# A float32 decoder layer on one core: parts of x1 side by side, five of seven products with both parts in one matmul, and the source's order on VectorE and ScalarE in two places

## The chip, the core and the metric

The kernel runs on one core of a Trainium2 chip. The metric is the device time of one execution in microseconds (us). TensorE multiplies matrices, VectorE and ScalarE do elementwise work, GpSimd here mostly issues DMAs, and SyncE issues the loads of weights. Each of these engines takes its instructions strictly in the order in which the program has them; one that waits holds all that stand behind it on its engine.

## The reference, cut to what matters

One layer for 512 tokens of width 2048, all in float32:

```python
h = rms_norm(x, attn_norm)
p = h @ w_in                                   # 2048 x 5632
y = concat(spatial_gating, short_conv, dilated_attention)   # all read p
x = x + y @ w_out                              # 2048 x 2048; this x is x1 below
h = rms_norm(x, mlp_norm)
x = x + square(relu(h @ w_mlp_in)) @ w_mlp_out # 2048 x 8192, then 8192 x 2048
```

## The kernel before

Every float32 product is made of three fp32r products: each operand is split into a high part (ScalarE copies it, rounding to fp32r, L242) and a low part (VectorE subtracts the high part, L243), and `mm3` (L154) issues high by high, high by low and low by high. The transposed tokens xT are held on 128 partitions, 16 slices of depth by 512 tokens. Weights come in pieces of two slices of depth (`load_w`, 128 x 2 x 512 numbers), three pieces deep: SyncE loads `wr`, ScalarE makes `wh`, VectorE makes `wl`.

`stream` (from L195 on) is one loop over all pieces of all groups. For piece i it loads piece i+2, issues the matmuls of piece i, and after each of the two slices takes one entry from a list of tasks (`step`); at a group's end it calls the group's `close`, which takes the results out of PSUM. There are six PSUM banks for this, and most groups use four. What is written there is the source's order. A scheduler then sets the order on each engine by its own estimate of times; a task that looks ready early is moved ahead.

The groups in order:

- **w_in**: four groups for q and k, and others. Together with the first group come the loads of xT (`xr`, `x_chunk`, split by `split_x`), and eight loads of x by token (`xn`, 512 KB each, issued on GpSimd) with a square on ScalarE each, for the first norm (`x_tokens`, `x_statistics`).
- **w_out**: its close adds x, which gives x1, and splits x1 times the gain into `xhl`: all high parts, and 32 KB per partition further on all low parts.
- **First product of the MLP** (w1, 8192 columns): a plain group of 512 columns; then 29 groups of 256 columns (`Strassen`), each by seven products of quarter size in place of eight, with 8 matmul steps each; then a plain group of 256 columns. The moving operands of the seven products are quarters of x1 or sums of them (`tt`). In three of the seven (`half` is None, L820) one weight load serves both parts: a matmul over 512 columns (high and low part of x1, 256 tokens each) and one over 256 (low part of the weights). In the other four, `mm3` issues three matmuls over 256 columns. The two parts come out in two halves of a bank and are added by VectorE.
- **Second product** (w2): four chunks of 2048 rows by four groups of 512 columns, each of 8 pieces (two slices of depth, four banks, three matmuls: 24 matmuls over 512 columns a piece, 192 a group). Its moving operand `hid` is made from the first product, read back from DRAM (`hs`, `hr`): `rest` in `hid_tasks` squares and multiplies on VectorE (L879, L880), copies on ScalarE, subtracts on VectorE, 64 times in all. Chunk 0's first half is made during the last group of w1, its second half during chunk 0's first group, and chunk c+1's during the second and third group of chunk c. `close_mlp_out` (L925) adds each bank to `acc`; only then is the bank free for the next group.

Quoted: the products of a Strassen group, and the task that makes one slice of `hid`.

```python
bank, half = ((0, None), (1, None), (2, 0), (3, None), (2, 1), (4, 0), (4, 1))[j]
...
if half is None:
    nc.tensor.matmul(pv, lhsT=h[:, m], rhs=b, start=start, stop=False)
    nc.tensor.matmul(pv[:, 1], lhsT=l[:, m], rhs=b[:, 0], start=False, stop=stop)
else:
    mm3(pv[:, half], (h[:, m], l[:, m]), (b[:, 0], b[:, 1]), start, stop)
...
def rest(n):
    t, k = room.pop(n), ks[n]
    nc.vector.scalar_tensor_tensor(out=t, in0=t, scalar=0.0, in1=t, op0=ALU.max, op1=ALU.mult)
    nc.vector.tensor_tensor(out=t, in0=t, in1=rbc, op=ALU.mult)
    split(d[:, 0, k], d[:, 1, k], t)
    load(n + ahead)
```

Of the kernel before, what the change touches and what calls it, by code (L numbers as in the profile page):

```python
# [9 lines left out]
F32 = mybir.dt.float32  # L10
# [30 lines left out]
def trunk_kernel(  # L41
# [46 lines left out]

    def step():
        if tasks:  # L90
            f = tasks.popleft()
            if f is not None:
                f()
# [28 lines left out]
    xh, xl = xhl[:, 0], xhl[:, 1]  # L122
    rstd = cpool.tile([P, TB], F32, name="rstd")
# [5 lines left out]
    def load_w(src, n, first=False):  # L129
# [5 lines left out]
        if first:  # L135
            for k in range(2):
                nc.sync.dma_start(out=first[0][:, k], in_=first[1][:, k])
                nc.sync.dma_start(out=raw[:, k], in_=src[:, k])
            for k in range(2):
                nc.vector.tensor_copy(out=h[:, k], in_=raw[:, k])  # L140
                split_x(k, first[0][:, k], g_attn)
                nc.vector.tensor_tensor(out=l[:, k], in0=raw[:, k], in1=h[:, k].bitcast(F32), op=ALU.subtract)
            return h, l
# [9 lines left out]
    def mm3(ps, a, b, start, stop):  # L153
        (ah, al), (bh, bl) = a, b  # L154
        nc.tensor.matmul(ps, lhsT=ah, rhs=bh, start=start, stop=False)  # L155
        nc.tensor.matmul(ps, lhsT=ah, rhs=bl, start=False, stop=False)  # L156
        nc.tensor.matmul(ps, lhsT=al, rhs=bh, start=False, stop=stop)  # L157
# [18 lines left out]
    def tr_group(src, nt, mov, close, order=None, before=None, tail=False):  # L176
# [13 lines left out]
        def mm(k, h, l, which=None):  # L190
            for n, (j, ts) in enumerate(parts):
                if which in (None, n):
                    s = slice(j * P, (j + 1) * P)
                    a, b = mov(order[k])
                    mm3(st[n][:, ts], (h[:, s], l[:, s]), (a[:, ts], b[:, ts]), k == 0, k == KT - 1)  # L195
# [49 lines left out]
    def split_x(k, src, gain):  # L245

        nc.scalar.activation(out=xh[:, k], in_=src, func=AF.Copy, scale=gain[:, k:k + 1])
        nc.vector.scalar_tensor_tensor(
            out=xl[:, k], in0=src, scalar=gain[:, k:k + 1], in1=xh[:, k].bitcast(F32), op0=ALU.mult, op1=ALU.subtract,
        )  # L250
# [13 lines left out]
    def x_tokens(i):  # L264
# [3 lines left out]
        nc.gpsimd.dma_start(out=xn_t, in_=xn_v[:, t, half * DH:(half + 1) * DH])  # L268
        return lambda: nc.scalar.activation(out=xn_t, in_=xn_t, func=AF.Square, accum_out=tok[:, t, half:half + 1])
# [104 lines left out]
    def x_chunk(kp):  # L374
# [6 lines left out]
        for n in range(2):  # L381
            split_x(2 * kp + n, xr[:, n], g_attn)
# [21 lines left out]
    def evac_qk(pss, which, half):  # L404
        gain = q_gain if which == 0 else k_gain
# [322 lines left out]
    def close_out(pss, ng):  # L728

        xg = mlp["xg"]  # L730
        for j in range(4):
# [7 lines left out]
            split_x(n, xg[:, n], g_mlp)  # L739
            tasks.append(lambda n=n: nc.scalar.activation(out=xg[:, n], in_=xg[:, n], func=AF.Copy, scale=g_mlp[:, n:n + 1]))  # L740
        if ng == 3:
            yc["cm"].__exit__(None, None, None)
            mlp["tcm"] = pool("sums")
            tt = mlp["tt"] = mlp["tcm"].__enter__().tile([P, 2, 4, KT // 2, TH], F32R, name="tt")
# [9 lines left out]
    def x_sums(tt, xv, m, j):  # L754
# [5 lines left out]
        split(tt[:, 0, j, s], tt[:, 1, j, s], out)  # L760

    def x_operand(j, m):

        if j < 3:
            k, t = ((0, 0), (1, 0), (1, 1))[j]
            return xhl[:, :, 2 * m + k, t * TH:(t + 1) * TH]
        return mlp["tt"][:, :, j - 3, m]

    class Strassen:
# [41 lines left out]
        def product(self, j, h, l):  # L811
            sp, i = mlp["spool"], self.i
            bank, half = ((0, None), (1, None), (2, 0), (3, None), (2, 1), (4, 0), (4, 1))[j]
# [16 lines left out]

            if j == 0:
# [3 lines left out]
                nc.scalar.copy(out=self.p[0], in_=pv[:, 0])  # L835
                add(self.p[0], pv[:, 1], self.p[0])
                return
            c = self.c
            if j == 1:
                add(c[:, 2], pv[:, 0], self.p[0])  # L840
                add(c[:, 2], pv[:, 1], c[:, 2])
            elif j == 2:
                add(c[:, 0], pv[:, 0], self.p[0])
            elif j == 3:
                nc.scalar.copy(out=self.p[1], in_=pv[:, 0])
                add(self.p[1], pv[:, 1], self.p[1])
            elif j == 4:
                add(c[:, 1], pv[:, 1], c[:, 0])
                add(c[:, 0:6:5], self.p[1].unsqueeze(1).broadcast_to([P, 2, TH]), c[:, 0:2])
            elif j == 6:  # L850
                add(c[:, 3:5], pv, c[:, 0:2])
                for n in range(2):
                    nc.gpsimd.dma_start(out=hd[self.c0 // P + n], in_=c[:, 2 + 2 * n:4 + 2 * n].rearrange("p h t -> p (h t)"))

    def close_mlp_in(pss, f0):

        for j, ps in enumerate(pss):
# [3 lines left out]
            nc.scalar.copy(out=c, in_=ps.rearrange("p (h t) -> p h t", h=2))  # L861
# [5 lines left out]
    def hid_tasks(c, ks, alloc, ahead):  # L867
# [9 lines left out]
        def rest(n):  # L877
            t, k = room.pop(n), ks[n]
            nc.vector.scalar_tensor_tensor(out=t, in0=t, scalar=0.0, in1=t, op0=ALU.max, op1=ALU.mult)  # L879
            nc.vector.tensor_tensor(out=t, in0=t, in1=rbc, op=ALU.mult)  # L880
# [7 lines left out]
    def open_last_in():  # L888
        mlp["tcm"].__exit__(None, None, None)
# [32 lines left out]
    def close_mlp_out(pss, ng):  # L922
        for j in range(4):
            dst = mlp["acc"][:, 4 * ng + j]
            nc.vector.tensor_tensor(out=dst, in0=pss[j], in1=dst, op=ALU.add)  # L925

    def close_last(pss, ng, j, ts):
        dst = mlp["acc"][:, 4 * ng + j, ts]
        nc.vector.tensor_tensor(out=dst, in0=pss, in1=dst, op=ALU.add)
# [22 lines left out]
    groups.append(tr_group(w1[:, :, :T], 4, xmov, lambda pss: close_mlp_in(pss, 0)))  # L952
    for c0 in range(T, DFF - 2 * P, 2 * P):
        groups.append(Strassen(c0))
    groups.append(tr_group(
        w1[:, :, DFF - 2 * P:], 2, xmov, lambda pss: close_last_in(pss, DFF // P - 2), before=open_last_in,
    ))
    for c in range(nch):
        for ng in range(4):
# [6 lines left out]
            ))  # L966
    stream(groups)
# [46 lines left out]
```

## Time and profile before

| | |
|---|---|
| median of 3 runs | 2099.56 us (2097.77 to 2105.01) |
| the profiled execution | 2101.5 us, of which the span from the first to the last instruction is 2099.8 us |
| TensorE busy | 98% of the span |
| VectorE busy | 55% of the span |
| ScalarE busy | 32% of the span |
| mean granted TensorE clock | 0.992 of full speed |

Busy time of TensorE counts matmuls that overlap, so 98% does not say that TensorE runs at its peak; what one matmul costs is read from the distance between the starts of two neighbours in the timeline. Waits of TensorE stand in the list of waits: who waited, for whom, us in total, how often, the longest.

### The profile page before, as it was taken

The numbers are of one execution on the slowest core, as the hardware profiler recorded it, in microseconds if no ns is written. First come the engines' busy times: TensorE is split into PE (matmuls) and PEld (weight loads), VectorE is DVE, ScalarE is ACT, GpSimd is POOL, SyncE is SP. The second block draws the span as 40 slices with busy tenths as digits, with TensorE's granted clock in tenths as the row PEclk, the third lists the DMA queues.
The fourth block names the chain that finished last, engine by engine and source line by source line (L and its number), as shares of the span: only waits on it lengthen the run. The fifth ranks groups of instructions, "written<-read, shape, count | busy, mean of one in ns | idle before, by whom it ended". The sixth has DMA issues, their size and how long they took to land.

```text
span 2099.8 us, 27447 instructions
## 1 busy us (share of the span) xinstructions
PE 2067.3 (98%) x11202; PEld 1807.8 (86%) x11202; DVE 1145.1 (55%) x1530; ACT 674.7 (32%) x905; POOL 100.6 (5%) x194
## 2 busy tenths in 40 slices
PE   9999999999999999999999999999989998999999
PEld 8999888888888889999999999977878887888888
DVE  5443453534335578878888788767372254322222
ACT  6233442322234434334333343432221222221221
POOL 1000000100000000000000000131010010000000
PEclk9999999999999999999999999999999999999999
DMA  8223222433533454444444444474343343233332
GB/s 276 90 76 111 71 71 68 128 96 96 188 119 126 125 161 131 131 140 122 140 131 124 138 131 126 127 254 151 112 150 96 95 133 112 92 101 97 114 120 81
DMA packets 247023, 259.81 MB, mean 124 GB/s; under 512 B 11748, under 2 KB 179940, under 8 KB 246896
## 3 DMA queue, kind: packets, MB, share of 16 engines
q1 hardware_dynamic: 229888, 206.08, 32.6%
q0 software_dynamic: 14560, 47.75, 6.5%
q10 hardware_dynamic: 2448, 4.23, 0.6%
q8 instruction: 88, 1.44, 0.3%
q14 instruction: 39, 0.32, 0.0%
HBM read 232.81 MB, written 25.19 MB: 123 GB/s over the span
## 4 chain that ended last, share of the span: by engine, by line
PE 79%; issue 16%; DMA 3%; POOL 1%; DVE 1%; SPq 0%; ACT 0%; POOLq 0%; DVEq 0%; ACTq 0%
PE pt L155 17%; PE pt L156 17%; PE pt L157 17%; PE pt L823 8%; PE pn L155 5%; PE pn L157 5%; PE pn L156 5%; PE pt L824 4%; DMA hs<-hd 1%; POOL hs L875 1%; DMA hd<-cn 1%; PE sc L505 0%; DMA wr<-in_w_in_dram 0%; PE et L518 0%; DVE wl L243 0%
## 5 line engine op out<-in xcount | busy, mean ns | idle before, releaser
L243 DVE TENSOR_TENSOR wl<-wr,wh 128x1024 fp32r<-128x1024 f32 (+2 forms) x287 | 321.4, 1120 | 652.8 <-ACT wh L242 596.5
L242 ACT CAST wh<-wr 128x1024 fp32r<-128x1024 f32 (+2 forms) x287 | 277.8, 968 | 799.6 <-PE pt L156 661.9
L155 PE MATMUL pt<-xhl,wh 128*128 128x512 f32 (+1 forms) x1144 | 419.6, 367 | 6.0 <-DVE acc L925 6.0
L156 PE MATMUL pt<-xhl,wh 128*128 128x512 f32 (+1 forms) x1144 | 418.3, 366 | 0.0
L157 PE MATMUL pt<-xhl,wl 128*128 128x512 f32 (+1 forms) x1144 | 418.1, 365 | 0.0
L155 PEld LDWEIGHTS pt<-xhl,wh 128*128 128x128 f32 x1144 | 216.5, 189 | 41.3 <-DVE acc L925 6.4
L157 PEld LDWEIGHTS pt<-xhl,wl 128*128 128x128 f32 x1144 | 216.4, 189 | 34.7
L156 PEld LDWEIGHTS pt<-xhl,wh 128*128 128x128 f32 x1144 | 216.6, 189 | 34.4 <-issue 0.2
L242 ACT CAST wh<-wq 128x1024 fp32r<-128x1024 f32 x145 | 152.0, 1048 | 250.7 <-PE pt L156 146.1
L243 DVE TENSOR_TENSOR wl<-wq,wh 128x1024 fp32r<-128x1024 f32 x145 | 177.0, 1221 | 91.2 <-ACT wh L242 91.1
L155 PE MATMUL pt<-hid,wh 128*128 128x512 f32 x512 | 201.7, 394 | 14.7 <-DVE acc L925 14.7
L157 PE MATMUL pt<-hid,wl 128*128 128x512 f32 x512 | 201.3, 393 | 2.1 <-DVE wl L243 2.0
L156 PE MATMUL pt<-hid,wh 128*128 128x512 f32 x512 | 201.2, 393 | 0.0
L155 PE MATMUL pt<-tt,wh 128*128 128x256 f32 x696 | 197.0, 283 | 0.3 <-DVE c L829 0.3
L157 PE MATMUL pt<-tt,wl 128*128 128x256 f32 x696 | 197.1, 283 | 0.0
L156 PE MATMUL pt<-tt,wh 128*128 128x256 f32 x696 | 197.0, 283 | 0.0
L155 PE MATMUL pn<-wh,xhl 128*128 128x384 f32 (+2 forms) x512 | 187.3, 368 | 4.4 <-DVE wh L140 3.8
L156 PE MATMUL pn<-wl,xhl 128*128 128x384 f32 (+2 forms) x512 | 180.4, 352 | 0.0
L157 PE MATMUL pn<-wh,xhl 128*128 128x384 f32 (+2 forms) x512 | 180.2, 352 | 0.0
L823 PE MATMUL pt<-xhl,wh 128*128 128x512 f32 x464 | 165.2, 398 | 0.0
L155 PEld LDWEIGHTS pt<-tt,wh 128*128 128x128 f32 x696 | 132.7, 191 | 3.1 <-issue 0.6
L157 PEld LDWEIGHTS pt<-tt,wl 128*128 128x128 f32 x696 | 132.9, 191 | 0.0
(210 smaller groups left out, 2933.5 us busy)
## 6 DMA issues: line engine op xcount, KB each, us to landing
wr<-in_w_mlp_out_dram SPq DMA_DIRECT2D x128, 512.0 KB, 3.6
wq<-in_w_mlp_in_dram SPq DMA_DIRECT2D x116, 512.0 KB, 4.1
wr<-in_w_in_dram SPq DMA_DIRECT2D x144, 128.0 KB, 2.4
wr<-in_w_out_dram SPq DMA_DIRECT2D x32, 512.0 KB, 3.6
hd<-c POOLq DMA_DIRECT2D x58, 256.0 KB, 2.6
hs<-hd POOLq DMA_DIRECT2D x56, 256.0 KB, 3.4
wr<-in_w_in_dram SPq DMA_DIRECT2D x24, 512.0 KB, 3.5
wr<-in_w_in_dram SPq DMA_DIRECT2D x31, 384.0 KB, 3.2
```

The costliest lines, as they stand in the source:

```text
L155: nc.tensor.matmul(ps, lhsT=ah, rhs=bh, start=start, stop=False)
L156: nc.tensor.matmul(ps, lhsT=ah, rhs=bl, start=False, stop=False)
L157: nc.tensor.matmul(ps, lhsT=al, rhs=bh, start=False, stop=stop)
L242: nc.scalar.copy(out=dst_h, in_=src)
L243: nc.vector.tensor_tensor(out=dst_l, in0=src, in1=dst_h.bitcast(F32), op=ALU.subtract)
L823: nc.tensor.matmul(pv, lhsT=h[:, m], rhs=b, start=start, stop=False)
L824: nc.tensor.matmul(pv[:, 1], lhsT=l[:, m], rhs=b[:, 0], start=False, stop=stop)
L875: nc.gpsimd.dma_start(out=room[n], in_=hd[c * KC + ks[n]])
```

## The change

Three things are done.

1. **Order.** `keep_in_program_order` makes an instruction keep the source's order on its engine. It is set for the VectorE and ScalarE work of splits, `rest`, `close_mlp_out`, `close_last`, `close_mlp_in` and the squares of `xn`, from the start of the stream until the first group closes, and again from the opening of the last group of w1 to the end. The eight `xn` loads are no longer issued ahead: task i issues load i, behind the last matmul that has been issued by then (`behind`), and square i-2. They begin with the sixth piece of the first group, one a piece.
2. **x1's parts side by side.** `xhl` is read as `x1v` in the first product of the MLP: for each slice and each half of the tokens 256 high parts and, right behind, 256 low parts, so a product with both parts reads 512 numbers in a row. The sums `tt` are laid out likewise. The two plain groups of w1 (288 matmuls over 512 columns) now read two runs of 256 numbers, 2 KB from the start of one to the start of the next (`x1mov`).
3. **Five products with both.** Products 0 to 4 of a Strassen group have one matmul over 512 columns and one over 256 for each step; products 5 and 6 keep three over 256. Products 2 and 4 get banks of their own, six in all, and one addition more each on VectorE (`take`).

```diff
+    def ordr(ins):
+        return tc.keep_in_program_order(ins) if ordered[0] else ins
...
+    x1v = xhl.rearrange("p s k t -> p (s k t)").rearrange("p (k h s t) -> p k h s t", k=KT, h=2, s=2)
...
+    def behind(ins):
+
+        tc.add_manual_dep(
+            ins.ins, last[0].ins.name, mybir.DependencyInfo(mybir.DependencyClass.Sync, mybir.DependencyReason.DATA),
+            reason="behind",
+        )
+        return ins
...
     def split(dst_h, dst_l, src):
-        nc.scalar.copy(out=dst_h, in_=src)
-        nc.vector.tensor_tensor(out=dst_l, in0=src, in1=dst_h.bitcast(F32), op=ALU.subtract)
...
+        ordr(nc.scalar.copy(out=dst_h, in_=src))
+        ordr(nc.vector.tensor_tensor(out=dst_l, in0=src, in1=dst_h.bitcast(F32), op=ALU.subtract))
...
-        squares = [x_tokens(i) for i in range(3)]
+        squares = []
 
         def one(i):
-            squares[i]()
-            if i + 3 < 2 * TB:
-                squares.append(x_tokens(i + 3))
-
-        for i in range(2 * TB):
+            if i < 2 * TB:
+                squares.append(x_tokens(i))
+            if i >= 2:
+                squares[i - 2]()
+
+        for i in range(2 * TB + 2):
             tasks.extend([lambda i=i: one(i), None])
         tasks.append(stat_columns)
...
     def evac_qk(pss, which, half):
+        ordered[0] = False
...
+    def x1mov(k):
+        return x1v[:, k, :, 0], x1v[:, k, :, 1]
...
-            bank, half = ((0, None), (1, None), (2, 0), (3, None), (2, 1), (4, 0), (4, 1))[j]
+            bank, half = j if j < 5 else 5, j - 5 if j >= 5 else None
...
+            def take(out, more):
+                add(out, pv[:, 0], more)
+                add(out, pv[:, 1], out)
...
             elif j == 2:
-                add(c[:, 0], pv[:, 0], self.p[0])
-            elif j == 3:
-                nc.scalar.copy(out=self.p[1], in_=pv[:, 0])
-                add(self.p[1], pv[:, 1], self.p[1])
+                take(c[:, 0], self.p[0])
             elif j == 4:
-                add(c[:, 1], pv[:, 1], c[:, 0])
+                take(c[:, 1], c[:, 0])
...
     def open_last_in():
+        ordered[0] = True
...
-            nc.vector.tensor_tensor(out=dst, in0=pss[j], in1=dst, op=ALU.add)
+            ordr(nc.vector.tensor_tensor(out=dst, in0=pss[j], in1=dst, op=ALU.add))
```

What it does to the order is seen at three places. **First, ScalarE at the start of the program.** `xr0` is the first chunk of xT with its two slices, `xn0` the first load by token, `wh2` and `wh3` the high parts of the second and third piece. Before:

```order
L115 ACTIVATE scr_82<-ones_75 128x1
L247 ACTIVATE xhl_93<-xr0_190,par_73 128x512
L269 ACTIVATE xn0_414,tok_99<-xn0_414 128x1024
L247 ACTIVATE xhl_93<-xr0_190,par_73 128x512
L247 ACTIVATE xhl_93<-xr1_206,par_73 128x512 x2
L242 CAST wh2_213<-wr2_212 128x2x384
```

Now:

```order
L120 ACTIVATE scr_82<-ones_75 128x1
L267 ACTIVATE xhl_93<-xr0_190,par_73 128x512 x2
L267 ACTIVATE xhl_93<-xr1_206,par_73 128x512 x2
L262 CAST wh2_213<-wr2_212 128x2x384
L267 ACTIVATE xhl_93<-xr2_218,par_73 128x512 x2
```

The square of `xn0` has gone from between the two slices of the first chunk; all eight squares stand behind `wh11`, the high part of the tenth piece.

**Second, VectorE at the end of the first group of the second product** (`pt265_0` to `_3` are its banks, `hs280` to `hs289` slices of `hid` for the next chunk, `wl275` to `wl277` low parts of the coming pieces). Before:

```order
L879 SCALAR_TENSOR_TENSOR hs287_12654<-hs287_12654 128x512
L880 TENSOR_TENSOR hs287_12654<-hs287_12654,rbc_96 128x512
L243 TENSOR_TENSOR xhl_93<-hs285_12618,xhl_93 128x512
L879 SCALAR_TENSOR_TENSOR hs289_12690<-hs289_12690 128x512
L243 TENSOR_TENSOR wl277_12502<-wr277_12500,wh277_12501 128x1024
L243 TENSOR_TENSOR xhl_93<-hs287_12654,xhl_93 128x512
L880 TENSOR_TENSOR hs289_12690<-hs289_12690,rbc_96 128x512
L925 TENSOR_TENSOR acc_12230<-pt265_0_12246,acc_12230 128x512
```

Now:

```order
L263 TENSOR_TENSOR wl275_12065<-wr275_12063,wh275_12064 128x1024
L263 TENSOR_TENSOR wl276_12095<-wr276_12093,wh276_12094 128x1024
L263 TENSOR_TENSOR wl277_12125<-wr277_12123,wh277_12124 128x1024
L956 TENSOR_TENSOR acc_11853<-pt265_0_11869,acc_11853 128x512
L956 TENSOR_TENSOR acc_11853<-pt265_1_11870,acc_11853 128x512
L956 TENSOR_TENSOR acc_11853<-pt265_2_11871,acc_11853 128x512
L956 TENSOR_TENSOR acc_11853<-pt265_3_11872,acc_11853 128x512
L263 TENSOR_TENSOR wl278_12159<-wr278_12157,wh278_12158 128x1024
L909 SCALAR_TENSOR_TENSOR hs280_12171<-hs280_12171 128x512
```

The whole work on the next chunk's slices now stands behind the additions that free the banks, one slice a piece.

**Third, VectorE at the start of that group** (`wl259`, `wl260`, `wl264`, `wl268` are the low parts of its first four pieces, `hr7` is the last slice of the first half of `hid`, `hs261` and `hs262` the first slices of the second half). Before:

```order
L243 TENSOR_TENSOR hid_12034<-hr7_12131,hid_12034 128x512
L243 TENSOR_TENSOR wl258_12157<-wr258_12155,wh258_12156 128x2x256
L243 TENSOR_TENSOR wl259_12179<-wr259_12177,wh259_12178 128x1024
L243 TENSOR_TENSOR wl260_12201<-wr260_12199,wh260_12200 128x1024
L243 TENSOR_TENSOR wl264_12242<-wr264_12240,wh264_12241 128x1024
L243 TENSOR_TENSOR wl268_12292<-wr268_12290,wh268_12291 128x1024
L879 SCALAR_TENSOR_TENSOR hs261_12234<-hs261_12234 128x512
```

Now:

```order
L910 TENSOR_TENSOR hr7_11754<-hr7_11754,rbc_96 128x512
L263 TENSOR_TENSOR hid_11657<-hr7_11754,hid_11657 128x512
L263 TENSOR_TENSOR wl264_11865<-wr264_11863,wh264_11864 128x1024
L909 SCALAR_TENSOR_TENSOR hs261_11857<-hs261_11857 128x512
L910 TENSOR_TENSOR hs261_11857<-hs261_11857,rbc_96 128x512
L263 TENSOR_TENSOR hid_11657<-hs261_11857,hid_11657 128x512
L909 SCALAR_TENSOR_TENSOR hs262_11859<-hs262_11859 128x512
L910 TENSOR_TENSOR hs262_11859<-hs262_11859,rbc_96 128x512
L263 TENSOR_TENSOR hid_11657<-hs262_11859,hid_11657 128x512
L263 TENSOR_TENSOR wl268_11915<-wr268_11913,wh268_11914 128x1024
```

`hr7` has moved from before `wl258` to between `wl260` and `wl264`, and two whole slices now stand ahead of `wl268`; the same holds for the pieces behind it. On ScalarE the copies that take the last w1 group out of PSUM (`cn`, L861) now stand behind the copy of `hr7`.

## Rows read from the trace of the kernel before

**Rows 1.** From the page: busy time, share of the span and instructions of each engine.

```profile
PE 2067.3 (98%) x11202; PEld 1807.8 (86%) x11202; DVE 1145.1 (55%) x1530; ACT 674.7 (32%) x905; POOL 100.6 (5%) x194
```

**Rows 2.** Waits of TensorE: who for whom, us in total, times, longest us.

```profile
PE pt L155 <- DVE acc L925: 20.7, 3, 7.5
PE pn L155 <- DVE wh L140: 3.8, 1, 3.8
PE pt L157 <- DVE wl L243: 2.0, 2, 1.1
```

**Rows 3.** Stretches: us, busy time of PE, PEld, DVE, ACT, POOL; granted clock, DMA share, GB/s.

```profile
12.00:17.40 5.40, 5.38 (x15) 4.78 (x16) 3.70 (x6) 2.89 (x4) 0.00 (x0) 0.50 0.86 308
...
1422.00:1427.00 5.00, 4.97 (x12) 3.91 (x13) 5.00 (x8) 0.97 (x2) 0.54 (x1) 0.50 0.60 178
...
1561.30:1567.00 5.70, 5.70 (x14) 4.44 (x15) 5.67 (x9) 0.98 (x2) 0.54 (x1) 0.50 0.50 167
```

**Rows 4.** Timeline of TensorE at the start: start, us, engine, line, operation [idle <-releaser].

```profile
7.89 0.34 PE L157 MATMUL pn<-wh,xhl 128*128 128x384 f32 x1
...
12.02 0.66 PE L155 MATMUL pn<-wh,xhl 128*128 128x384 f32 x1 [3.78 <-DVE wh L140]
...
16.55 1.26 PE L155 MATMUL pn<-wh,xhl 128*128 128x384 f32 x4
```

**Rows 5.** DMAs issued in the first 3 us: queue, count, KB each, median us to landing.

```profile
xn<-in_xn_dram POOLq DMA_DIRECT2D x3, 512.0 KB, 8.9
```

**Rows 6.** Timeline of TensorE where the first bank is waited for.

```profile
1414.14 0.40 PE L157 MATMUL pt<-hid,wl 128*128 128x512 f32 x1
...
1422.03 0.80 PE L155 MATMUL pt<-hid,wh 128*128 128x512 f32 x1 [7.49 <-DVE acc L925]
```

**Rows 7.** Timeline of VectorE, ScalarE and GpSimd around the last w1 group.

```profile
1345.51 0.68 DVE L243 TENSOR_TENSOR wl<-wr,wh 128x512 fp32r<-128x512 f32 x1
...
1351.42 0.69 DVE L879 SCALAR_TENSOR_TENSOR hr<-hr 128x512 f32<-128x512 f32 x1 [1.62 <-DMA hr<-hd]
...
1352.15 0.69 DVE L880 TENSOR_TENSOR hr<-hr,rbc 128x512 f32<-128x512 f32 x1
...
1357.69 0.62 ACT L242 CAST hid<-hr 128x512 fp32r<-128x512 f32 x1 [1.26 <-DVE hr L880]
...
1358.35 0.69 DVE L243 TENSOR_TENSOR hid<-hr,hid 128x512 fp32r<-128x512 f32 x1
...
1366.00 0.59 ACT L861 COPY cn<-pt 128x512 f32<-128x512 f32 x1 [1.21 <-PE pt L157]
...
1372.94 1.61 POOL L875 DMA_DIRECT2D hs<-hd  x3 [4.08 <-DMA hd<-cn]
...
1375.95 1.29 DVE L879 SCALAR_TENSOR_TENSOR hs<-hs 128x512 f32<-128x512 f32 x2 [1.75 <-DMA hs<-hd]
...
1382.19 1.22 DVE L243 TENSOR_TENSOR wl<-wr,wh 128x1024 fp32r<-128x1024 f32 x1
```

**Rows 8.** Timeline of TensorE: three of 256 columns, pairs of 512 and 256, 512 alone.

```profile
1300.04 0.28 PE L155 MATMUL pt<-xhl,wh 128*128 128x256 f32 x1
...
1301.48 0.28 PE L155 MATMUL pt<-xhl,wh 128*128 128x256 f32 x1
...
1304.72 0.40 PE L823 MATMUL pt<-xhl,wh 128*128 128x512 f32 x1
...
1309.67 0.40 PE L823 MATMUL pt<-xhl,wh 128*128 128x512 f32 x1
...
1359.68 0.39 PE L155 MATMUL pt<-xhl,wh 128*128 128x512 f32 x1
...
1366.48 0.39 PE L155 MATMUL pt<-hid,wh 128*128 128x512 f32 x1
```

**Rows 9.** Groups of VectorE by shape: busy us, mean ns of one, idle before and releaser.

```profile
L829 DVE TENSOR_TENSOR c<-pt,p 128x256 f32<-128x256 f32 x58 | 24.2, 417 | 1.0 <-PE pt L157 0.7 <-PE pt L824 0.3
```

**Rows 10.** The stretch of the 29 Strassen groups, columns as in rows 3.

```profile
764.00:1344.00 580.00, 579.69 (x4175) 547.08 (x4174) 477.37 (x558) 228.55 (x263) 34.55 (x65) 1.00 0.43 130
```

More of the change, by code (lines that the diff above doesn't have):

```diff
@@ L139, in load_w @@
             for k in range(2):
-                nc.vector.tensor_copy(out=h[:, k], in_=raw[:, k])
-                split_x(k, first[0][:, k], g_attn)
-                nc.vector.tensor_tensor(out=l[:, k], in0=raw[:, k], in1=h[:, k].bitcast(F32), op=ALU.subtract)
+                ordr(nc.vector.tensor_copy(out=h[:, k], in_=raw[:, k]))
+                split_x(xh[:, k], xl[:, k], first[0][:, k], g_attn[:, k:k + 1])
+                ordr(nc.vector.tensor_tensor(out=l[:, k], in0=raw[:, k], in1=h[:, k].bitcast(F32), op=ALU.subtract))
             return h, l
@@ L156, in mm3 @@
         nc.tensor.matmul(ps, lhsT=ah, rhs=bl, start=False, stop=False)
-        nc.tensor.matmul(ps, lhsT=al, rhs=bh, start=False, stop=stop)
+        last[0] = nc.tensor.matmul(ps, lhsT=al, rhs=bh, start=False, stop=stop)
+    last = [None]
+    def behind(ins):
[4 more added lines that the diff above has]
+        return ins
     def pieces_of(src, n, order):
@@ L241, in split, with split_x @@
     def split(dst_h, dst_l, src):
[L242 to L250 removed]
+        ordr(nc.scalar.copy(out=dst_h, in_=src))
+        ordr(nc.vector.tensor_tensor(out=dst_l, in0=src, in1=dst_h.bitcast(F32), op=ALU.subtract))
+    def split_x(dst_h, dst_l, src, gain):
+        ordr(nc.scalar.activation(out=dst_h, in_=src, func=AF.Copy, scale=gain))
+        ordr(nc.vector.scalar_tensor_tensor(
+            out=dst_l, in0=src, scalar=gain, in1=dst_h.bitcast(F32), op0=ALU.mult, op1=ALU.subtract,
+        ))
     def rsqrt(dst, v, s, y):
@@ L267, in x_tokens @@
         xn_t = p0.tile([P, DH], F32, tag="xn", name=f"xn{i}", bufs=3)
-        nc.gpsimd.dma_start(out=xn_t, in_=xn_v[:, t, half * DH:(half + 1) * DH])
-        return lambda: nc.scalar.activation(out=xn_t, in_=xn_t, func=AF.Square, accum_out=tok[:, t, half:half + 1])
+        behind(nc.gpsimd.dma_start(out=xn_t, in_=xn_v[:, t, half * DH:(half + 1) * DH]))
+        return lambda: ordr(nc.scalar.activation(
+            out=xn_t, in_=xn_t, func=AF.Square, accum_out=tok[:, t, half:half + 1]))
     def stat_columns():
@@ L759, in x_sums @@
         nc.vector.tensor_tensor(out=out, in0=a, in1=b, op=ALU.subtract)
-        split(tt[:, 0, j, s], tt[:, 1, j, s], out)
+        split(tt[:, j, s, 0], tt[:, j, s, 1], out)
     def x_operand(j, m):
@@ L860, in close_mlp_in @@
             c = cc[:, 2 * (j % 2):2 * (j % 2) + 2]
-            nc.scalar.copy(out=c, in_=ps.rearrange("p (h t) -> p h t", h=2))
+            ordr(nc.scalar.copy(out=c, in_=ps.rearrange("p (h t) -> p h t", h=2)))
             nc.gpsimd.dma_start(out=hd[f0 + j].rearrange("p (h t) -> p h t", h=2), in_=c)
```

40 lines of the change are left out of this document (24 added, 16 removed).

## The prediction

> **What bounds the kernel now.** The page's busy line comes first [rows 1]: TensorE 98%, VectorE 55%, ScalarE 32%. TensorE sets the time, so a change gains where it shortens TensorE's own work, takes away a wait of TensorE, or spares it a stretch at the lower clock. The list of waits says how much waiting there is [rows 2]: three long ones for `acc`, 20.7 us, one of 3.8 at the start, and two small ones for `wl`, 2.0. [...] That is about all there is to win beside the matmuls themselves: 20.7 + 2.0 + 8.2 = 30.9 in the second product, 3.8 + 2.7 = 6.5 at the start.
>
> **The start.** The first matmuls of the second slice wait until 12.02, those of the first having begun their last at 7.89, and the next piece begins at 16.55 [rows 4]. Beside the pieces that TensorE waits for, three loads `xn` of 512 KB were issued in the first 3 us [rows 5]. The engines of the DMA moved 308 GB/s in the first stretch of [rows 3]; at that rate 3 x 512 KB are 5.1 us of transfer. The change takes them out of the way until the sixth piece, so the second slice can land some 5 us earlier, enough for the 3.78 us of [rows 4] to go. Then its 12 matmuls over 384 columns run at the full clock: 12 x 0.17 = 2.0 us (0.17 being 384/512 of the 0.2267 worked out below) instead of 16.55 - 12.02 = 4.5. Together 6.3. SyncE's loads of the following pieces may now be what is late, so I take **-6.0**; bounds -3 (half of the gain is eaten by the next load) and -6.7 (the half clock of the 0.85 up to 17.40 goes too). The squares come later by pieces of the first group, and with them the norm's statistics; no wait of TensorE for these is among the rows, so I cost that at nothing. What covers it are the groups for q and k that run in between; if it doesn't, a wait of about a piece's length, 2 to 4 us, comes back. It lies within the bound of -3.
>
> **The second product, its three waits.** At the first of them TensorE stands from 1414.14 to 1422.03 [rows 6], because the additions that free a bank stand on VectorE behind slices of the next chunk (the order before, in the section on the change). Now they stand directly behind the low part of the second next piece. The whole 30.9 goes, if nothing else is late then. In the later groups VectorE has per piece one slice and one low part. By [rows 7] a slice is 0.73 for the square (1351.42 to 1352.15), the same again for the multiplication, 0.66 for ScalarE's copy (1357.69 to 1358.35) and 0.69 for the subtraction, 2.81 in all; a low part of 1024 numbers is 1.22. That is 4.0 us of VectorE per piece of TensorE, which is 24 x 0.2267 = 5.44: the distance of two matmuls over 512 columns is (1366.48 - 1359.68)/30 = 0.2267 [rows 8]. So VectorE has 1.4 us to spare in each piece, and four additions of 0.7 begin in time.
>
> **The second product, a new wait.** At its beginning the same order costs. During the last group of w1 a piece of TensorE is 12 x 0.2267 = 2.72, but VectorE has, in a fixed row, a slice and a low part of half size, 2.81 + 0.68 = 3.49. Eight such pieces from 1345.5 [rows 7] end at 1373.4, and `hr7`'s copy on ScalarE some 0.7 before that. Behind this copy stand now the copies `cn` that take the group's result out; one of them ran at 1366.00, now at about 1373.1. The result goes to DRAM and comes back as `hs261`, whose square began at 1375.95, 10 us after the copy; it becomes 1383.0. Now `wl268`, the low part of the fourth piece, stands behind two whole slices, and the high part, on ScalarE, behind their copies. TensorE wants this piece at 1366.5 + 3 x 5.44 = 1382.8. The high part can be there when two slices but for the last subtraction and its own second have passed, 1383.0 + 2 x 2.81 - 0.7 + 1 = 1388.3: a wait of 5 to 6 us. The three pieces behind it have the same: eight slices and three low parts end at 1383.0 + 22.5 + 3.7 = 1409.2, where TensorE would want the seventh piece at 1366.5 + 6 x 5.44 = 1399.1. So TensorE comes out of this about 10 us late, in several waits; a lower clock inside that stretch costs little more, since VectorE sets the pace there. Net for the second product -30.9 + 10 = **-20.9**. The bounds: -31 if the new wait doesn't come, -14 if it is 17 with a half clock stretch behind it as after the waits of [rows 3]. I take -20.9, because each step has its row and no slack is left in them.
>
> **Five pairs.** 29 groups of 8 steps, two more products with both: 464 steps have a matmul over 512 and one over 256 in place of three over 256. Three cost 0.360 ((1301.48 - 1300.04)/4), thus 0.120 each; a pair now costs (1309.67 - 1304.72)/14 = 0.3536 [rows 8]. A pair whose 512 columns lay in a row should cost 0.2267 + 0.120 = 0.3467. So it is 0.0069 above that, and what differs is that its moving columns are two runs of 256, 32 KB apart in the partition (the plain matmuls of 0.2267 read one run). If laying them side by side gives these 6.9 ns back, 464 x 0.0133 = 6.2 us are gained on the new pairs and 29 x 8 x 3 x 0.0069 = 4.8 on the three that were pairs before: **-11.0**. If it doesn't: 464 x 0.0064 = -3.0. I take -11.0, since no other difference in shape is in the rows. [...]
>
> In turn 288 matmuls of the plain groups of w1 (192 and 96) now read two runs, 2 KB apart: 288 x 0.0069 = **+2.0**, or nothing if the jump is not what costs. The 58 additions more on VectorE are 417 ns each [rows 9], 24.2 us. In that stretch VectorE is busy 477 of 580 us [rows 10]; it would be 502 of 569, 88%. What hides them is that stretch's slack, 2.3 us for each of 29 groups; the sixth bank was free before. I cost them at nothing; without the cover it is up to +24.
>
> **Sum.** -6.0 - 20.9 - 11.0 + 2.0 = -35.9 against the profiled 2101.5: 2065.6. The median of the runs is 1.9 below the profiled execution, so **2064** as a median.
>
> **The rivals.**
>
> - *The jump costs nothing*: the 6.9 ns belong to changing between 512 and 256 columns, and stay. Then -3.0 in place of -11.0 and no +2.0: -29.9, **2070**. For it: the pairs before differ from plain matmuls in that also. [...] Against: one run against two is the plainer difference.
> - *The new wait doesn't come*, because slices overlap more than one after the other, or loads come back earlier: 10 us better, **2054**. For it: pairs of slices ran interleaved at 1375.95 before (one row holds two squares). Against: program order forbids that now.
> - *The new wait is larger or the start gives nothing*: waits as after the old ones, each with a half clock stretch of 5.7 behind it, two more of them and -3 at the start: **2078 to 2082**.
> - *VectorE becomes the bound of the 29 groups*: its additions stand in the way of TensorE's banks and the stretch grows by the 24.2 instead of shrinking by 11: -6.0 - 20.9 + 24.2 + 2.0 = -0.7, **2099**, no change. For it: 88% busy and ScalarE's copies in between. Against: TensorE waits for nothing worth a row in that stretch now.
> - *Slower: VectorE in a strict row becomes the bound of the second product.* Place: the 48 pieces in which slices for a next chunk are made. It decides from 1.4 us of waiting (for a slice read back from DRAM, for ScalarE) per piece; each microsecond above costs 48. With 2.5 us of it, +53 on 2066: **2119**. For it: waits of 1.62 and 1.26 stand in [rows 7]. Against: 1.26 is mostly ScalarE's copy, already in the 2.81, and the slices are loaded ahead.
>
> **How the numbers follow.** Forecast 0.42; the jump that costs nothing 0.25; no new wait 0.15; larger waits 0.10; no change 0.05; slower 0.03. About 0.3%, 6.3 us, is what a measurement can tell from no change. So faster 0.92, same 0.05, slower 0.03. The range from 2052 to 2082 takes in the first four cases with the bounds of the start (3), the waits (+7, -10) and the pairs (+8 less 2).
>
> **What would show it.** Right: the first item after the start at about 10.5 instead of 16.55 and no half clock there; no wait for `acc` in the list, but waits for `wh` or `wl` of 5 us or more in the first group of the second product; a pair at 0.347 and matmuls of the plain w1 groups at 0.234; the stretch of 29 groups 11 us shorter. Wrong: a pair still at 0.354, waits for slices or banks in the Strassen stretch, or a wait for `wl` in groups 2 and 3 of a chunk.

## The result and the profile after

The changed kernel takes 2066.95 us (2066.42 to 2067.64), the kernel before, run beside it, 2098.66: a ratio of 0.9843, 95% interval 0.9823 to 0.9863. That is 1.6% faster, clear of the spread of the executions, as forecast, and 3 us above the 2064 of the forecast. The profiled execution took 2066.42 with a span of 2064.7, 35.1 shorter than the span before. By medians the gain is only 31.7: the profiled execution of before (2101.5) was 2.8 above its median, that of after 0.5 below. So of the 3 us by which the median missed the forecast, 0.8 lies in the forecast's sum (2065.6 for the profiled execution) and the rest in its last step, which took 1.9 off for the median. First the page's busy line and the list of TensorE's waits, to be held against [rows 1, 2] (waiting, for whom, us in total, times, longest):

```profile
PE 2052.0 (99%) x10738; PEld 1776.3 (86%) x10738; DVE 1173.0 (57%) x1588; ACT 677.7 (33%) x905; POOL 100.6 (5%) x194
...
PE pt L162 <- ACT wh L262: 6.2, 2, 5.1
PE pn L162 <- DVE qn L440: 1.3, 2, 0.7
```

Before, the row for `qn` was:

```profile
PE pn L155 <- DVE qn L416: 0.6, 1, 0.6
```

The waits for `acc` are gone, a new one for the high part of a piece is there. TensorE has 464 matmuls less: three over 256 columns have become two, 464 times.

The span can be cut at four points that both traces have: the first matmul of the second piece, the first pair of the first Strassen group, the first matmul with `hid`, and the end. The forecast's +2.0 for the plain groups of w1 is split by their 192 and 96 matmuls.

| | before | after | difference | forecast |
|---|---|---|---|---|
| up to the second piece | 16.55 | 9.99 | -6.56 | -6.0 |
| up to the first Strassen group, the row above included | 764.54 | 758.85 | -5.69 | -6.0 + 1.3 = -4.7 |
| the 29 groups and the last group of w1 | 601.94 | 594.95 | -6.99 | -11.0 + 0.7 = -10.3 |
| second product | 733.3 | 710.9 | -22.4 | -20.9 |
| span | 2099.8 | 2064.7 | -35.1 | -35.9 |

The start, in TensorE's timeline (start, us, engine, line, operation) and as a stretch (busy times, granted clock, DMA share, GB/s), answering to [rows 4] and to the first of [rows 3]:

```profile
7.48 0.34 PE L162 MATMUL pn<-wh,xhl 128*128 128x384 f32 x1
7.91 0.44 PE L163 MATMUL pn<-wl,xhl 128*128 128x384 f32 x1
...
9.99 0.97 PE L162 MATMUL pn<-wh,xhl 128*128 128x384 f32 x4
...
12.00:17.40 5.40, 5.40 (x33) 5.40 (x32) 4.47 (x6) 3.54 (x6) 0.00 (x0) 1.00 0.95 319
```

The second slice follows the first with a pause of 0.3 us in place of 3.78, the second piece starts at 9.99, and where the clock was 0.50 it is 1.00, with 33 matmuls instead of 15 in the same stretch. Some 0.9 us of this is given back before the first Strassen group; 0.7 of it stands in the list of waits, where `qn` rose from 0.6 to 1.3.

The first group of the second product, in the timelines of VectorE, ScalarE and TensorE, and the stretch behind the wait:

```profile
1362.43 1.23 DVE L263 TENSOR_TENSOR wl<-wr,wh 128x1024 fp32r<-128x1024 f32 x1 [1.23 <-ACT wh L262]
1369.79 0.69 DVE L909 SCALAR_TENSOR_TENSOR hs<-hs 128x512 f32<-128x512 f32 x1 [6.13 <-DMA hs<-hd]
...
1375.59 1.23 DVE L263 TENSOR_TENSOR wl<-wr,wh 128x1024 fp32r<-128x1024 f32 x1 [0.25 <-ACT wh L262]
...
1359.86 0.62 ACT L262 CAST hid<-hr 128x512 fp32r<-128x512 f32 x1 [2.62 <-DVE hr L910]
1360.38 1.07 ACT L891 COPY cn<-pt 128x512 f32<-128x512 f32 x2
...
1374.51 1.04 ACT L262 CAST wh<-wr 128x1024 fp32r<-128x1024 f32 x1
...
1375.61 0.80 PE L162 MATMUL pt<-hid,wh 128*128 128x512 f32 x1 [5.09 <-ACT wh L262]
...
1375.60:1382.50 6.90, 6.89 (x19) 5.50 (x20) 5.21 (x8) 2.18 (x3) 4.57 (x9) 0.59 0.78 254
```

This is the new wait, link by link: the copies `cn` stand behind the copy of the last `hr` (1359.86, then 1360.38; TensorE had finished the group at 1353.8), the first `hs` comes back at 1369.79, VectorE having stood idle for 6.13 us, two whole slices go ahead of the low part at 1375.59, and their copies go ahead of the high part at 1374.51, for which TensorE waits 5.09 us at the fourth piece. The granted clock in the stretch behind it is 0.59 in the mean, 0.50 up to 1381.00.

The Strassen groups: the stretch in which they lie, then the first pair of three groups in a row (their distance is the length of a group), and three pairs each in the second and the third group.

```profile
758.85:1332.00 573.15, 573.15 (x3713) 521.94 (x3712) 491.34 (x605) 228.76 (x263) 34.00 (x64) 1.00 0.44 131
...
778.73 0.40 PE L851 MATMUL pt<-xhl,wh 128*128 128x512 f32 x1
...
779.08 0.40 PE L851 MATMUL pt<-xhl,wh 128*128 128x512 f32 x1
...
780.14 0.40 PE L851 MATMUL pt<-xhl,wh 128*128 128x512 f32 x1
...
798.63 0.40 PE L851 MATMUL pt<-xhl,wh 128*128 128x512 f32 x1
...
799.33 0.39 PE L851 MATMUL pt<-xhl,wh 128*128 128x512 f32 x1
...
800.37 0.39 PE L851 MATMUL pt<-xhl,wh 128*128 128x512 f32 x1
...
818.25 0.40 PE L851 MATMUL pt<-xhl,wh 128*128 128x512 f32 x1
```

One group takes 19.90 us (778.73 to 798.63), the next 19.62 (to 818.25), and so on in turn; 14 of the 29 take 19.62. In the slow ones a pair costs 0.353 (779.08 to 780.14, three pairs), as before the change; in the fast ones 0.347 (799.33 to 800.37), the price that the forecast had for all. VectorE is busy 491 of 573 us, and TensorE waits for nothing worth a row there: the cover for the additions held.

The plain groups of w1 read two runs now, and that costs nothing: (1353.80 - 1347.00)/30 = 0.2267, as in [rows 8].

```profile
1347.00 0.39 PE L162 MATMUL pt<-xhl,wh 128*128 128x512 f32 x1
...
1353.80 0.39 PE L162 MATMUL pt<-hid,wh 128*128 128x512 f32 x1
```

### The profile page after: what moved, and what is told of

The parts are those of the page before. It is cut to its first block, busy times and chain, and to the rows that moved or that the text cites. A ratio compares the mean times of both kernels' runs of the same rounds, so it can differ in the third digit from the quotient of the medians.

```text
span 2064.7 us, 26522 instructions
## 1 busy us (share of the span) xinstructions
PE 2052.0 (99%) x10738; PEld 1776.3 (86%) x10738; DVE 1173.0 (57%) x1588; ACT 677.7 (33%) x905; POOL 100.6 (5%) x194
## 4 chain that ended last, share of the span: by engine, by line
PE 97%; issue 1%; DMA 1%; DVE 0%; POOL 0%; ACT 0%; SPq 0%; POOLq 0%; ACTq 0%
PE pt L162 20%; PE pt L164 20%; PE pt L163 20%; PE pt L851 13%; PE pt L852 7%; PE pn L162 5%; PE pn L163 5%; PE pn L164 5%; PE sc L529 0%; PE et L542 0%; PE qt L463 0%; DMA acc<-x1d 0%; DMA wr<-in_w_in_dram 0%; PE po L164 0%; PE po L163 0%
## 5 line engine op out<-in xcount | busy, mean ns | idle before, releaser
L851 PE MATMUL pt<-tt,wh 128*128 128x512 f32 x696 | 245.0, 395 | 0.0
L852 PE MATMUL pt<-xhl,wl 128*128 128x256 f32 x464 | 130.1, 280 | 0.0
```

## The experiments

Three things were to be told apart: what the layout does and what the row of products does; which part of the order makes the new wait; and what it was at the start that made room. Each kernel is the changed one with the edit that is shown.

**The layout alone (e1), the number of pairs alone (e2).**

```diff
 e1:
-    x1v = xhl.rearrange("p s k t -> p (s k t)").rearrange("p (k h s t) -> p k h s t", k=KT, h=2, s=2)
+    x1v = xhl.rearrange("p s k (h t) -> p k h s t", h=2)
 ... and tt as [P, 2, 4, KT // 2, TH] again
 e2:
-            bank, half = j if j < 5 else 5, j - 5 if j >= 5 else None
+            bank, half = ((0, None), (1, None), (2, 0), (3, None), (2, 1), (4, 0), (4, 1))[j]
 ... and add in place of take for products 2 and 4
```

> The changed kernel with x1's parts back 32 KB apart (in x1 and in the sums), five products with both. In the changed kernel the 29 Strassen groups take 573.2 us and alternate between 19.62 us (a pair of matmuls 0.347) and 19.90 us (a pair 0.353). Theory 1, lying side by side is what lets a pair run at 0.347: here no group reaches 19.62, all take 19.90, the stretch 577.1 us, so 3.9 more. Theory 2, the row of products alone (five pairs, then two by three) brings the two speeds, the layout nothing: the groups alternate as before, 573.2 us. Theory 3, that of the prediction (the jump costs 6.9 ns in each of 1160 pairs): 573.2 + 8.0 = 581 us. The last group of w1, which reads one run here and two in the changed kernel, takes 21.77 us in the changed kernel: the same here by theories 1 and 2, 0.7 us less by theory 3.

> The changed kernel with three products with both instead of five, x1's parts side by side. Theory 3 (each pair is 6.9 ns cheaper by the layout): the 29 groups take 580.2 - 4.8 = 575.4 us, 19.84 a group. Theory 1 (side by side helps only in some groups or products): between 575.4 and 580.2 us, with some of the pairs at 0.347 and others at 0.353. Theory 2 (the layout gives nothing): 580.2 us, 19.99 a group, as in the kernel before.

First pairs of groups 2, 3 and 4 of e1, then of groups 2 and 3 of e2:

```profile
798.89 0.40 PE L851 MATMUL pt<-xhl,wh 128*128 128x512 f32 x1
...
818.51 0.40 PE L851 MATMUL pt<-xhl,wh 128*128 128x512 f32 x1
...
838.41 0.40 PE L851 MATMUL pt<-xhl,wh 128*128 128x512 f32 x1
```

```profile
800.17 0.40 PE L851 MATMUL pt<-xhl,wh 128*128 128x512 f32 x1
...
820.16 0.40 PE L851 MATMUL pt<-xhl,wh 128*128 128x512 f32 x1
```

With the parts 32 KB apart again the groups alternate between 19.62 and 19.90 as with the parts side by side; the whole takes 2066.91 us. With three pairs side by side they take 19.99, as before the change, and the whole 2073.85. So theory 2 holds, and the jump that the prediction charged 6.9 ns for costs nothing: at 32 KB (e1) and at none (the changed kernel) the groups take 19.62 and 19.90, and at 2 KB a plain matmul takes 0.2267 as with one run. The gain comes from the pairs alone, and half of the groups let them run at their fast price.

**What sets the price of a pair (e7, e8).** e7 puts one matmul, whose result is overwritten, ahead of some groups; e8 makes all seven products pairs from the third group on.

```diff
 e7:
+            if j == 0 and 4 <= g < 24:
+                n = (16, 48, 64, 80, 128, 144, 192, 256, 272, 288)[(g - 4) // 2]
+                nc.tensor.matmul(ps[:, :n], lhsT=h[:, 0], rhs=..., start=True, stop=True)
 e8:
+            seven = (self.c0 - T) // (2 * P) >= 2
+            bank, half = (j, None) if seven or j < 5 else (5, j - 5)
...
+            elif seven and j >= 5:
+                take(c[:, j - 2], c[:, j - 5])
```

> The changed kernel with one matmul more (its result is overwritten) ahead of the first product of groups 4 to 23: over 16, 48, 64, 80, 128, 144, 192, 256, 272 and 288 columns, each size in two groups in a row; groups 0 to 3 and 24 to 28 as they are. Theory P1 (a pair runs at 0.347 or 0.353 by a phase of TensorE against its weight loads that the matmuls before it leave behind): some sizes turn the state, so that both groups of such a size run at 0.347 (19.62 us and the added matmul) or the row of fast and slow groups breaks; a size of 256, one more of the kind that precedes it, changes nothing. Rival P2 (the alternation follows something else that changes by group, such as buffers or addresses): fast and slow groups go on alternating, even groups fast, whatever the size.

> The changed kernel with all seven products with both (the seventh bank from the two that nothing uses in that stretch) from the third Strassen group on; the first two as they are, since the second of them leaves TensorE in the state in which pairs run at 0.347. Theory P1 (the state lasts as long as pairs follow pairs): 27 groups of 56 x 0.347 = 19.4 us, all of them, the 29 take 564 us instead of 573.2, 2058 us. Rival P2 (by the group): half of the groups at 56 x 0.353 = 19.8, 569 us, 2063 us. Rival V (VectorE, with 530 of 564 us, becomes the bound): groups of 20 us or more with waits for banks or weights.

In e7 (2070.11 us in all) both groups behind 272 and both behind 288 columns are fast. Here the added matmul and the first pairs around the first of them:

```profile
1118.04 0.40 PE L856 MATMUL pt<-xhl,wh 128*128 128x512 f32 x1
...
1138.05 0.40 PE L856 MATMUL pt<-xhl,wh 128*128 128x512 f32 x1
...
1157.93 0.29 PE L849 MATMUL pt<-xhl,wh 128*128 128x272 f32 x1
1158.06 0.39 PE L856 MATMUL pt<-xhl,wh 128*128 128x512 f32 x1
...
1177.80 0.39 PE L856 MATMUL pt<-xhl,wh 128*128 128x512 f32 x1
...
1197.54 0.39 PE L856 MATMUL pt<-xhl,wh 128*128 128x512 f32 x1
```

The groups behind 256 columns take 20.01 (from 1118.04, with the matmul that is added to the next one), those behind 272 take 19.74 (1158.06 to 1177.80 to 1197.54). All eight groups behind 128 to 256 columns are slow, and both behind 64; at 16, 48 and 80 one of the two is fast. So in these groups the alternation is no matter of buffers or addresses: what TensorE has run just before changes it. e11 (below), which is edited at the start of the program only, shows the same without an added matmul, since the row of fast and slow groups is shifted by one there: its second group takes 19.62 and its third 19.90, the other way round than in the changed kernel.

```profile
779.65 0.40 PE L851 MATMUL pt<-xhl,wh 128*128 128x512 f32 x1
...
799.27 0.40 PE L851 MATMUL pt<-xhl,wh 128*128 128x512 f32 x1
...
819.17 0.40 PE L851 MATMUL pt<-xhl,wh 128*128 128x512 f32 x1
```

That 256 would change nothing was wrong; without the matmul one of those two groups would have been fast. In e8 the fast price stays once it is there (third group, fourth, last):

```profile
798.73 0.40 PE L852 MATMUL pt<-xhl,wh 128*128 128x512 f32 x1
...
818.16 0.39 PE L852 MATMUL pt<-xhl,wh 128*128 128x512 f32 x1
...
1303.49 0.39 PE L852 MATMUL pt<-xhl,wh 128*128 128x512 f32 x1
```

(1303.49 - 798.73)/26 = 19.41 a group, for all of them; 2057.36 us in its one execution, 9.6 less than the changed kernel. VectorE's two further additions a group are hidden too.

**The order in the second product (e3, e4, e5).** e3 begins it later, e4 leaves it out there, e5 exempts the two copies `cn`.

```diff
 e3, e4:
     def open_last_in():
-        ordered[0] = True
 e3 only:
     def close_mlp_out(pss, ng):
+        ordered[0] = True
 e5:
-            ordr(nc.scalar.copy(out=c, in_=ps.rearrange("p (h t) -> p h t", h=2)))
+            nc.scalar.copy(out=c, in_=ps.rearrange("p (h t) -> p h t", h=2))
```

> The changed kernel, but the source's order on VectorE and ScalarE begins only when the first group of the second product closes, not at the opening of the last group of w1. Theory A (the fixed row of slices and low parts in the last w1 group and the first group makes the new wait, 10.0 us with what follows): the first chunk falls from 184.1 us to between 174.1 and 177 us, no wait for the high parts of 5 us, no wait for the banks, 2057 us in all. Rival B (the wait is that of the result that goes to DRAM and back, whatever the order): a wait of 4 to 7 us stays in the first group, first chunk 182 to 185 us, 2065 us. Rival C (the order in the first group is needed for the banks at its end): the wait for the first bank comes back, 5 to 8 us and a stretch at half the clock behind it.

> The changed kernel without the source's order in the second product (it holds at the start of the program only). Theory: the three waits for the banks come back with their half clock; chunks of 187.3, 183.1 and 184.3 us as in the kernel before instead of 184.1, 174.1 and 174.1, so 22.4 us more, 2087 us. Rival: the new row of Strassen groups shifts the scheduler's estimates, so that less than half of it comes back, under 2076 us.

> The changed kernel; only the two copies on ScalarE that take the last group of w1 out of PSUM don't keep the source's order, the rest of it does. Theory A1 (6 to 7 us of the new wait come from these copies standing behind the copy of the last slice of the first half): the copies run at 1354 to 1356 instead of 1360.4, the first chunk is 184.1 - 6.8 = 177.3 us, no wait above 3.5 us in it, 2058 us in all. Rival A2 (two whole slices ahead of each low part make the wait, whenever the copies run): the first chunk stays at 182 us or above.

The waits of TensorE in the second product, of e3, of e4 and of e5, and ScalarE's copy in e5:

```profile
PE pt L164 <- DVE wl L263: 1.9, 1, 1.9
```

```profile
PE pt L162 <- DVE acc L955: 21.2, 3, 7.7
PE pt L164 <- DVE wl L263: 3.0, 1, 3.0
```

```profile
PE pt L162 <- ACT wh L262: 2.7, 3, 1.2
...
PE pt L164 <- DVE wl L263: 0.5, 1, 0.5
...
1354.66 1.27 ACT L891 COPY cn<-pt 128x512 f32<-128x512 f32 x2 [0.28 <-PE pt L164]
```

The first three chunks, from first matmul to first matmul; the whole time is a median for the first two rows and one execution for the others:

| | chunk 0 | chunk 1 | chunk 2 | whole, us |
|---|---|---|---|---|
| before | 187.27 | 183.07 | 184.34 | 2098.66 |
| changed | 184.10 | 174.08 | 174.08 | 2066.95 |
| e3, order from the first close | 176.23 | 174.08 | 174.08 | 2059.48 |
| e4, no order there | 189.00 | 182.81 | 183.73 | 2089.88 |
| e5, `cn` exempt | 179.10 | 174.08 | 174.08 | 2062.74 |

e4 gives back 4.90 + 8.73 + 9.65 = 23.3 us: the order in the second product is worth that, and nothing else of the change helps there. e3 keeps all of it and pays for 2.15 of the first group's 10.0 us, so theory A holds: the fixed row in the last w1 group and the first group makes the new wait, while the banks need the order only from the first close. e5 shows the share of the copies: they run 0.5 us before the first matmul with `hid` (1354.66 against 1355.14) where they ran 6.6 behind it (1360.38 against 1353.80), and the chunk is 5.0 us shorter, somewhat less than the 6.8 expected. The other 5.0 belong to the two slices ahead of each low part: in e5 these low parts start 6.9 us apart on VectorE (1371.97, 1378.87, 1385.76), while a piece of TensorE is 5.44, and each of three pieces in a row comes 1.45 late.

**The start (e6, e11).** e6 lets the first three loads by token go at once as before, all else as changed; e11 keeps the loads back, but drops the order at the start.

```diff
 e6:
-        behind(nc.gpsimd.dma_start(out=xn_t, ...))
+        (behind if i > 2 else (lambda q: q))(nc.gpsimd.dma_start(out=xn_t, ...))
 e11:
-    ordered[0] = True
     stream(groups)
```

> The changed kernel with the first three loads by token issued at the start as before; the order on VectorE and ScalarE, squares included, stays as changed. Theory S1 (the loads' share of the DMA makes the second half of the first piece late): TensorE waits 3 to 4 us before the second slice, the second piece begins at 15.5 to 17 us instead of 9.99, half the clock behind the wait, 6 us more: 2072 us. Rival S2 (the square between ScalarE's copies, now gone, was what was late): the second piece begins before 11 us, 2067 us.

> The changed kernel without the source's order at the start of the program; the loads by token still wait for the sixth piece. Theory S1 (the loads' share of the DMA is all that counts): the second piece begins at 10 to 11 us, 2067 us. Rival S2 (the order is needed too): one of the squares gets between the pieces' copies on ScalarE, and the second piece begins after 12 us.

TensorE's timeline of e6, then of e11:

```profile
11.57 0.66 PE L162 MATMUL pn<-wh,xhl 128*128 128x384 f32 x1 [3.81 <-DVE wh L147]
...
16.29 1.48 PE L162 MATMUL pn<-wh,xhl 128*128 128x384 f32 x4
```

```profile
10.54 0.87 PE L162 MATMUL pn<-wh,xhl 128*128 128x384 f32 x4
```

With the early loads the wait is back, 3.81 us (VectorE, whose high part TensorE waits for, itself waits 5.02 us for the load of these weights), the second piece begins at 16.29, the whole takes 2073.03. Without the order it begins at 10.54, the whole takes 2067.28. The loads are the cause (S1); the order at the start moves half a microsecond at most.

**A version drawn from these (e9, e10, e12).** e9: e8 for all groups, one matmul over 288 columns ahead of the first, and e3's order. e10: the changed kernel with seven pairs in all groups, nothing ahead. e12: e9, and the loads of x1 into `acc` held back behind the matmuls of the group that needs them (for the first group: until its later pieces).

```diff
 e12:
-            for n in range(4 * ng, 4 * ng + 4):
-                nc.gpsimd.dma_start(out=mlp["acc"][:, n], in_=x1d[n])
+            def fetch(n):
+                behind(nc.gpsimd.dma_start(out=mlp["acc"][:, n], in_=x1d[n]))
+
+            for n in range(4 * ng, 4 * ng + 4):
+                tasks.append(lambda n=n: fetch(n)) if ng == 0 else fetch(n)
```

> Drawn from the runs so far: all seven products with both in all 29 groups, one matmul over 288 columns (overwritten) ahead of the first of them, and the source's order in the second product only from the close of its first group. Theory P1 (the state is set by the matmuls ahead and lasts): all 29 groups at 19.41 us, 563 us; the first chunk at 176 us instead of 184.1; against the changed kernel's 2066.95 that is -9.1 -1.0 -7.9: 2049 us. Rival: the two gains get in each other's way, since the scheduler's estimates of the last w1 group shift with the new groups; then 2053 us or more.

> The changed kernel with seven products with both in all 29 groups and nothing ahead of the first. Theory P1 (the slow state lasts as long as pairs follow pairs, too): all groups at 56 x 0.353 = 19.78 us, the 29 in 573.7 us against 563 to 564 with the fast state. Rival P3 (pairs alone always settle into 0.347, and the products in three matmuls are what brings the slow state back): 19.41 us from the second or third group on, 564 us.

> The one before the last two, with the loads of x1 into acc issued behind the matmuls of the group that needs them, so that they don't share the DMA with the first slices of the second product. Theory: the one wait of 2 us that was left in the first group with the later order came from slices landing late beside these loads; it goes, the first chunk takes 174.1 to 175 us, 2047 us. Rival: the slices land as late as before (three buffers hold them back), the first chunk stays at 176 us; or the additions now wait for these loads and banks come late, 178 us or more.

First pairs of the second and the last group of e9, of e10 and of e12:

```profile
778.60 0.40 PE L855 MATMUL pt<-xhl,wh 128*128 128x512 f32 x1
...
1312.84 0.40 PE L855 MATMUL pt<-xhl,wh 128*128 128x512 f32 x1
```

```profile
778.47 0.39 PE L852 MATMUL pt<-xhl,wh 128*128 128x512 f32 x1
...
1302.63 0.39 PE L852 MATMUL pt<-xhl,wh 128*128 128x512 f32 x1
```

```profile
778.70 0.39 PE L855 MATMUL pt<-xhl,wh 128*128 128x512 f32 x1
...
1302.86 0.39 PE L855 MATMUL pt<-xhl,wh 128*128 128x512 f32 x1
```

Over 27 groups e9 takes 19.79 a group, e10 and e12 19.41. e9's expectation fell: the matmul over 288 columns, which had helped behind the products of three, did nothing behind the plain group, and e9's trace shows the slow price from end to end: 2060.13 us (2058.4 to 2061.4). Its first chunk took 178.47 us, not 176, with one wait of 2.5 for a low part and a granted clock of 0.93 in the mean from 1375 to 1400. e10 went as P3 said, against P1: nothing was put ahead, yet its first group turned fast at its fourth product and all others were fast, 2056.92 in its one execution. e12's trace turned at the same place. But P3 doesn't hold either, since e9's pairs never settled into the fast price. What holds in all of them is less: once a whole group of pairs has run at one price, the groups behind it run at the same. e12 took 2046.68 us in the profiled execution and 2057.0 to 2057.6 in four others, a distance of 10.5. The 29 groups take 573.8 in e9's trace and 563.2 in e12's, 10.6 apart, so these four probably ran at the slow price, but they have no trace. e9 and e12 issue the same matmuls in the same order, so their row alone doesn't set the price; something that differs from execution to execution counts too. One thing in the traces goes with the turn. In the fourth product of the first group VectorE ends the low part of the weights 0.68 us before the first matmul that reads it in e9, which stayed slow, and only 0.27 before in e12 and 0.24 in e10, which turned. In e11 TensorE waited for it, and the pairs right behind ran at 0.347:

```profile
768.40 0.39 PE L852 MATMUL pt<-tt,wl 128*128 128x256 f32 x1 [0.20 <-DVE wl L263]
```

But in e1 and e5 it ended 0.13 and 0.27 before, and their first groups stayed slow. So a late low part is a candidate that no run tested, and the cause stays open.

What e12 was made for is settled: the first chunk takes 174.08 us where e9 took 178.47, like the two chunks behind it, with no wait for slices or weights. So that wait came from the loads of x1 into `acc`. e12's median is 2057.22, ratio 0.9795 (0.9778 to 0.9811) to the kernel before: better than the changed kernel, and by another 10 us whenever the fast price holds, by the times in one execution of five. e8 and e10 ran once each, so how often they get the fast price isn't known. e12 with e8's first two groups, from which the third one enters fast, wasn't tried.

## Why the prediction was right, point by point

- **The start, -6.0.** The mechanism and its size were right: 5.1 us of transfer (3 x 512 KB at the 308 GB/s of [rows 3]) out of the way, no wait, a granted clock of 1.00 in place of 0.50; -6.56 at the second piece, and e6, which brings only the early loads back, costs 6.1. Some 0.9 is given back later. That the squares come later was priced at nothing; if it is what made `qn` wait, it costs 0.7.
- **The three waits for `acc`, -30.9.** They went with their half clock: the granted clock is 1.00 from 1383.00 to the end of the third chunk (1886.06). No row is named for the 8.2 in the 30.9 and the 2.7 in the 6.5 at the start; what the trace of before shows is a granted clock of 0.50 over 5.0, 5.7 and 5.7 us behind the three waits (from 1422.00, 1561.30 and 1745.60) and over 5.4 us at the start (from 12.00), and halves of these are 8.2 and 2.7. By the chunks they had cost 13.19 + 8.99 + 10.26 = 32.4 above 174.08; the prediction's sum had missed 1.5 of it.
- **The new wait, +10.** Measured 184.10 - 174.08 = 10.0. The prediction had the place (fourth piece), the chain (`hr7`'s copy, `cn`, `hs261`, two slices, high part) and the first wait (5 to 6 us, measured 5.09; its sum 1383.0 + 2 x 2.81 - 0.7 + 1 is 1388.9, not 1388.3, so by its own terms 6.1). It also had the end: VectorE's row lets the seventh piece start at 1396.29, where TensorE would have wanted it at 1353.8 + 6 x 5.44 = 1386.4, 9.9 late against 10.1. e5 splits it in halves between the copies and the slices.
- **Five pairs, -11.0, and x1mov, +2.0: this step failed**, in its cause and in its size. "No other difference in shape is in the rows" passed over the one that the first rival named, the change between 512 and 256 columns, and the two runs don't matter at all (19.62 and 19.90 in e1 too). By that rival it would have been -3.0 and no +2.0; measured is -7.0, since half of the groups run their 40 pairs at 0.347 all the same: per group 20.0 becomes 19.90 or 19.62, and 14 x 40 x 0.0069 = 3.9 comes on top of the 3.0. So the number came out between forecast and rival, and for neither's reason. The rows held no plain matmul with two runs and no pair with one, so nothing there told the two candidates apart; with even chances for them the forecast would have been their middle, 2067, which is near the result by chance only.
- **VectorE's additions at nothing.** Right; even at 519 of 563 us (e12) they were hidden.
- **The sum.** -5.7 - 22.4 - 7.0 = -35.1 against -35.9. The pairs missed by 4.0 and the start by 0.3; the +2.0 that never came and 1.5 more in the second product made up for most of it. That the sum came out so near is luck.

## What to carry to other kernels

A strict order on an engine is worth setting from the point at which a late instruction holds up something scarce (here a PSUM bank), and not earlier: set two groups earlier it lined up copies and slices ahead of weights and cost 10 us of the 32 it saved. Before the first matmuls, loads that nobody needed yet cost about their transfer time here: 6.1 us (e6) for an estimated 5.1 of transfer, with the granted clock at 0.50 from 12.00 to 17.40, behind the wait. A difference in price between two shapes has as many candidates as the shapes differ in; the cheapest test of a layout is the layout alone.

## What the runs showed of the hardware that was not expected

- At a granted clock of 1.00 a matmul over 512 columns follows the one before after 226.7 ns (changed kernel, 1347.00 to 1353.80), one over 256 after 120.0 ([rows 8]). A pair of both takes either 346.7, their sum, or 353.3 (changed kernel, from 799.33 and from 779.08), and with nothing but pairs it stayed at one of these for 27 groups of 56 pairs: 19.41 us a group in e12, 19.79 in e9, which issue the same matmuls in the same order.
- Which of them it is depends in part on what TensorE ran just before: in e7, behind products of three matmuls, an extra one over 272 or 288 columns gave the fast price in four groups of four, one over 128 to 256 the slow one in eight of eight. Behind a plain group one over 288 columns was followed by the slow price in e9 and, through e12's first three products, too; what turned e12 isn't known.
- Moving operands in one run of 512 numbers or in two of 256, 2 KB or 32 KB apart, cost the same to within the resolution of the rows (0.2267 plain in the kernel before and in the changed one; groups of 19.62 and 19.90 in pairs in the changed kernel and in e1).
